# Rows of 128 extra bytes between the split activations and weights of a float32r transformer trunk

## The chip, the cores and the metric

The kernel runs on one core of a Trainium2 chip (trn2). The metric is the device time of one execution in microseconds (us). Two runs of the kernel before took 1998.0 and 1999.53 us, median 1998.76 us. TensorE (PE) multiplies, VectorE (DVE) and ScalarE (ACT) work elementwise, GpSimd (POOL) does a few elementwise steps, and SyncE (SP) issues all DMAs.

## The reference, cut to what matters

Two layers of a bidirectional encoder on 512 tokens of width 1024, all in float32. Each layer is FFN, token mixing, FFN, each behind an RMS norm with a shift, a scale and a gate that come from a conditioning vector.

```python
def swiglu(h, wi, wo):
    gate, up = jnp.split(h @ wi, 2, axis=-1)
    return (jax.nn.silu(gate) * up) @ wo
...
    for l in range(DEPTH):
        mod = (c_act @ ada_w[l] + ada_b[l]).reshape(b, N_MOD, 1, D_MODEL)
...
        h = modulate(rmsnorm(x, norm_ffn1[l]), sh1, sc1)
        x = x + 0.5 * g1 * swiglu(h, ffn1_wi[l], ffn1_wo[l])
        h = modulate(rmsnorm(x, norm_mix[l]), sh2, sc2)
        x = x + g2 * token_mixing(h, cos, sin, w_in[l], sink[l], onorm_a[l], onorm_b[l], w_out[l])
        h = modulate(rmsnorm(x, norm_ffn2[l]), sh3, sc3)
        x = x + 0.5 * g3 * swiglu(h, ffn2_wi[l], ffn2_wo[l])
    return rmsnorm(x, final_norm)
```

`token_mixing` projects h to queries, keys and values (`w_in`), attends in 16 heads, and projects back (`w_out`). D_FF is 2816, that is 22 tiles of 128.

## The kernel before

Activations lie feature-major: a tile holds 128 features in its partitions and the 512 tokens along the row. Each float32 operand of a large product is split into two float32r parts, a high one and the rest, and `mm3` makes a product of three matmuls: high weight by high activation (line 149), low weight by high activation (line 150), high weight by low activation (line 151). The weights are stationary (a load of 128x128, which the trace shows apart as PEld, one per matmul), the activations are the moving operand.

The tiles in question are these:

- `hi` and `lo` (lines 124, 125 and 736): the two parts of one weight chunk, 1024 float32r per partition, six buffers each in the pool `wp`. A chunk holds up to 8 stationary blocks of 128 columns, so its blocks lie 512 bytes apart.
- `hh0..7` and `hl0..7` (lines 209, 210): the two parts of the normed activations, 512 columns, one buffer each in the pool `hp`. They are moving operands of the FFN's first product and of the mixer's projections. In the projection of the values (lines 451 to 453) it is the other way round: `hi` and `lo` move, 320 columns at a time, and `hh`, `hl` are stationary.
- `gh0..7` and `gl0..7` (lines 361, 362): the two parts of the gated activations of the FFN, 512 columns, in the pool `ffn` that is opened anew for each FFN. They are the moving operands of the FFN's second product.

`yh` and `yl` (line 641) are the attention's second half; they take the slots of `hh` and `hl` in `hp`, with 512 columns. `yah` and `yal` (line 648) are the first half, in the pool `mix`.

Within a pool the tiles lie one behind the other. Their rows are 4096 or 2048 bytes, whole multiples of 512, so all tiles of a pool begin at the same remainder. In the program as built, `hi`, `lo`, `hh` and `hl` begin at multiples of 256 bytes (`hi` at 53504, 57600, ..., `hh0` at 102656), and all tiles of the pools `ffn` and `mix` begin 128 bytes beyond one (`gh0` at 188032).

An FFN runs in three thirds of 7, 7 and 8 hidden tiles: first the products with `wi`, whose two results give `gh` and `gl` of a hidden tile (`take`), then the eight output tiles (`out_tiles`). Where a norm follows, the last output tiles and the first tiles of the next phase (`group`) run by token halves, 256 columns at a time. Each engine runs its instructions in the order in which the scheduler wrote them.

Of the kernel before, what the change touches and what calls it, by code (L numbers as in the profile page):

```python
# [11 lines left out]
F32R = mybir.dt.float32r  # L12
# [6 lines left out]
KD = 8  # L19
# [39 lines left out]
def tile_trunk(ctx: ExitStack, tc: tile.TileContext, xT, c, positions, adaT, cols, sink, wi1, wo1,  # L59
# [25 lines left out]
    snk = const.tile([128, L * 8], F32, name="snk")  # L85
    nsnk = const.tile([128, L * 8], F32, name="nsnk")

    # weight stream: every chunk is loaded once, in the order of use, and split into two float32r parts
    specs = []
    finer = set()  # L90
    live = {}
# [24 lines left out]
    def emit_chunk(pieces=1):  # L116
        i = state["emit"]
        if i >= len(specs):
            return
        state["emit"] += 1  # L120
        ap = specs[i]
        n = ap.shape[1]
        raw = wp.tile([128, 1024], F32, tag="raw", name="raw", bufs=2)
        hi = wp.tile([128, 1024], F32R, tag="hi", name="hi")
        lo = wp.tile([128, 1024], F32R, tag="lo", name="lo")
        nc.sync.dma_start(raw[:, :n], ap)
        step = 512 if i in finer else n
        for a in range(0, n, step):
            sl = slice(a, min(a + step, n))
            A.activation(hi[:, sl], raw[:, sl], AF.Copy)  # L130
            V.tensor_tensor(lo[:, sl], raw[:, sl], hi.bitcast(F32)[:, sl], op=ALU.subtract)  # L131
        live[i] = (hi, lo)
# [21 lines left out]
    HALF = (slice(0, HS), slice(HS, S))  # L154

    def rsqrt(out, src, n, scale):
        """(src * scale + EPS) ** -0.5: an integer guess and two steps of third order; the constant factor of
        both steps is in the argument."""
        v, t, y, q = (tiny.tile([128, 8], F32, tag=f"r{i}", name=f"r{i}")[:, :n] for i in range(4))
        V.tensor_scalar(v, src, scale * RK, EPS * RK, op0=ALU.mult, op1=ALU.add)  # L160
        V.tensor_scalar(y.bitcast(I32), v.bitcast(I32), -0.5, float(0x5F3759DF), op0=ALU.mult, op1=ALU.add)
        for ca, cb, o in ((RA, RB, y), (RA / RQ, RB / RQ ** 2, out)):
            V.tensor_tensor(t, y, y, op=ALU.mult)
            V.tensor_tensor(t, t, v, op=ALU.mult)
            V.scalar_tensor_tensor(q, t, -ca, t, op0=ALU.add, op1=ALU.mult)
            V.scalar_tensor_tensor(o, q, cb, y, op0=ALU.add, op1=ALU.mult)
# [3 lines left out]
    class Norm:  # L170
# [35 lines left out]
            self.R[h] = p  # L206

        def alloc(self):
            self.h = [(hp.tile([128, S], F32R, tag=f"hh{k}", name=f"hh{k}"),
                       hp.tile([128, S], F32R, tag=f"hl{k}", name=f"hl{k}")) for k in range(KD)]  # L210

        def make(self, k, h, gs, sh, s=None):
            s = s or HALF[h]
# [8 lines left out]

    temps = [None, None]

    # adaLN: one column of the modulation per 128 outputs
    ada_list = []
    ada = {}

# [46 lines left out]
        ada["cs"] = cs  # L275

    def group(norm, gs, sh, n):
        """First n output tiles of a phase, contraction outermost, so that they follow the norm."""
        Ws = [chunk() for _ in range(n)]
        ps = [pm.tile([128, S], F32, tag="mm", name="mm") for _ in range(n)]  # L280
        if not norm.h:
            norm.alloc()
        for k in range(KD):
            if k >= norm.made:
                norm.make(k, 0, gs, sh)
            for W, p in zip(Ws, ps):
                mm3(p[:, HALF[0]], W, k, norm.h[k], HALF[0], k == 0, k == KD - 1)
            if k == KG[0]:
                with tc.high_priority(offset=HG):
                    norm.stat(1)  # L290
            if k == KG[1]:
                norm.bcast(1)
        for k in range(KD):
            norm.make(k, 1, gs, sh)
        for W, p in zip(Ws, ps):
            for k in range(KD):
                mm3(p[:, HALF[1]], W, k, norm.h[k], HALF[1], k == 0, k == KD - 1)
            yield p
            ahead()
# [7 lines left out]

    def out_tiles(jobs, kts, X, gate, norm, step=None, skew=SKEW, at=((0, 5), (2, 3)),
                  final=None, mod=None):
        """jobs: (m, weights, first k tile of them). The last ones run by token halves when a norm follows."""  # L310
        n = len(jobs)
        for q in range(n - skew if norm else n):
            m, W, w0 = jobs[q]()
            p = pm.tile([128, S], F32, tag="mm", name="mm")
            for k in range(kts):
                mm3(p, W, w0 + k, X[k], FULL, k == 0, k == kts - 1)
            resid(p, m, gate, FULL, norm, None, final)
            ahead()
            if step:
                step()  # L320
        if norm:
            last = [jobs[q]() for q in range(n - skew, n)]
            ps = [pm.tile([128, S], F32, tag="mm", name="mm") if q < 4 else
                  pq.tile([128, S], F32, tag="s", name="mm") for q in range(skew)]
            ahead(AH)
            for h in range(2):
                for j, (m, W, w0) in enumerate(last):
                    for k in range(kts):
                        if h == 1 and (j, k) == at[0]:
                            with tc.high_priority(offset=HP):  # L330
                                norm.stat(0)
                        if h == 1 and (j, k) == at[1] and not final:
                            norm.bcast(0)
                            norm.alloc()
                            for m2 in range(PRE):
                                norm.make(m2, 0, *mod)
                                norm.made += 1
                        mm3(ps[j][:, HALF[h]], W, w0 + k, X[k], HALF[h], k == 0, k == kts - 1)
                    with tc.high_priority(offset=HP):
                        with tc.issue_after(norm.first) if h and j == skew - 1 and norm.made else nullcontext():  # L340
                            resid(ps[j], m, gate, HALF[h], norm, h if j == skew - 1 and h in TAIL[bool(final)] else None, final)

    def ffn(l, sub, norm, pool, step, start=None, final=None, mod=None):
# [3 lines left out]
        for ti, (f0, n) in enumerate(THIRDS):  # L347
# [3 lines left out]
            def take(p):  # L351
                pend.append(p)
                if len(pend) < 2:
                    return
                pg, pu = pend
                pend.clear()
                sg = pool.tile([128, S], F32, tag="sg", name="sg", bufs=2)
                A.activation(sg, pg, AF.Silu)  # L358
                V.tensor_tensor(sg, sg, pu, op=ALU.mult)  # L359
                j = len(g)  # L360
                gh = pool.tile([128, S], F32R, tag=f"gh{j}", name=f"gh{j}")
                gl = pool.tile([128, S], F32R, tag=f"gl{j}", name=f"gl{j}")
                A.activation(gh, sg, AF.Copy)  # L363
                V.tensor_tensor(gl, sg, gh.bitcast(F32), op=ALU.subtract)  # L364
                g.append((gh, gl))
# [25 lines left out]
    def mixer(l, norm, pool, mod):  # L391
# [150 lines left out]
                yield n  # L542

        def heads_(makers, after):
            """The heads' steps, each head's scores a head ahead of its values."""
            cur = makers[0]()
            for qt in range(4):
                cur.scores(qt)
# [19 lines left out]
                cur = nxt  # L568

        def weave(main, fills):  # L570
            """Steps of main with fills[i] = (first head, generator, us of it per step) from that head on."""
            due = 0.0
            i = 0
            for n in main:
                if i + 1 < len(fills) and n >= fills[i + 1][0]:
                    for _ in fills[i][1]:
                        pass
                    i += 1
                    due = 0.0
                due += fills[i][2]  # L580
                while due > 0:
                    d = next(fills[i][1], None)
                    if d is None:
                        break
                    due -= d
            for _ in fills[i][1]:
                pass
# [106 lines left out]
        out_tiles(jobs(), 4, ya, gate, nxt, None, MSK, MAT, mod=mod)  # L694
        return nxt

    # ---- start
    FP = dict(bufs=1, reuse_waits="tile")
    first = ctx.enter_context(ExitStack())
    pool = first.enter_context(tc.tile_pool(name="ffn", **FP))  # L700
# [3 lines left out]
    make_identity(nc, ident)  # L704

    def warm(n):
        """Products that nobody reads: the array's clock follows its activity."""
        p = pm.tile([128, S], F32, tag="mm", name="warm")
        for _ in range(n):
            T.matmul(p[:, :128], ident, ident, start=True, stop=True)  # L710
# [19 lines left out]
    def start():  # L730
        n = 6
        Ws = []
        for j in range(n):
            raw = wp.tile([128, 1024], F32, tag="raw", name="raw", bufs=2) if j < 2 else \
                pool.tile([128, 1024], F32, tag=f"raw{j}", name="raw")
            hi, lo = (wp.tile([128, 1024], F32R, tag=t, name=t) if j < 6 else
                      pool.tile([128, 1024], F32R, tag=t, name=t) for t in ("hi", "lo"))
            Ws.append((raw, hi, lo))
        ps = [pm.tile([128, S], F32, tag="mm", name="mm") if j < 4 else pq.tile([128, S], F32, tag="s", name="mm")
              for j in range(n)]  # L740
# [61 lines left out]
        ada_step()  # L802
    first.close()
    def final_out(norm, xgs, pool):
        """The last norm: the tiles with their gain go back to token-major and take the tokens' factors there."""
        for h in range(2):
            ps = []
            for t in range(2):
# [133 lines left out]
```

## Time and profile before

| what | value |
|---|---|
| median of two runs | 1998.76 us |
| span of the profiled execution, first to last instruction | 1996.3 us |
| PE busy | 98% of the span, 10016 matmuls |
| DVE, ACT, POOL busy | 59%, 38%, 5% |
| mean granted TensorE clock | 0.995 of full speed |

The profiled execution's own time is its span, and the median of the runs is 2.5 us longer; work ahead of the first and behind the last instruction lies in that difference. A matmul's record starts when its moving operand begins to stream and ends when its last result is out, so records of neighbours overlap. The time that a matmul costs in a stream is therefore the distance from its start to the next one's start, called the spacing below, and not the length of its record.

### The profile page before, as it was taken

The page shows a single profiled execution, that of the slowest core. Times are in us where ns is not written, and L with a number is a line of the kernel's source. Part 1 is how long each engine was busy: PE and PEld are TensorE (multiplying, and loading weights), DVE is VectorE, ACT ScalarE, POOL GpSimd, SP SyncE. Part 2 cuts the span into 40 slices and gives each one's busy share as a digit, 9 for nine tenths or more (in the row PEclk, how much of TensorE's full clock was granted, in tenths as well). Part 3 has the DMA queues.
Part 4 walks back from the last instruction along what each step waited for, and adds up shares of the span by engine and source line. Part 5 has one row for each costly group of instructions (what it writes and reads, how often), then busy time and mean ns, then how long its engine had stood idle before and what let it go on. Part 6 is the DMA issues. An engine that isn't in the chain of part 4 may idle for free.

```text
span 1996.3 us, 25904 instructions
## 1 busy us (share of the span) xinstructions
PE 1965.7 (98%) x10016; PEld 1654.3 (83%) x10016; DVE 1169.7 (59%) x2130; ACT 750.9 (38%) x1332; POOL 91.8 (5%) x69
## 2 busy tenths in 40 slices
PE   7999999999999999999999999999999999999998
PEld 5888888898778888888898888889877898888887
DVE  7978433576798888733473333337678973333333
ACT  4422222355685422222242222224557752222223
POOL 4000000021200000000000000000121000000000
PEclk8999999999999999999999999999999999999999
DMA  7788333244413698633233223331543123332331
GB/s 255 277 302 330 132 100 101 84 109 122 126 38 112 219 332 322 238 96 104 85 96 92 98 96 97 100 98 59 153 110 102 54 77 101 102 97 92 104 95 43
DMA packets 84942, 266.97 MB, mean 134 GB/s; under 512 B 10706, under 2 KB 13906, under 8 KB 84820
## 3 DMA queue, kind: packets, MB, share of 16 engines
q1 hardware_dynamic: 84820, 265.33, 40.8%
q8 instruction: 79, 1.29, 0.3%
q14 instruction: 43, 0.35, 0.0%
HBM read 244.31 MB, written 2.10 MB: 123 GB/s over the span
## 4 chain that ended last, share of the span: by engine, by line
PE 90%; DVE 4%; DMA 2%; issue 2%; ACT 1%; SPq 0%; POOL 0%; DVEq 0%; ACTq 0%; POOLq 0%
PE mm L151 26%; PE mm L149 26%; PE mm L150 26%; PE ptr L512 2%; PE po L519 1%; PE po L520 1%; PE s L482 1%; PE s L483 1%; DVE lo L131 1%; PE mm L451 1%; PE mm L453 1%; PE mm L452 1%; PE p L527 1%; DVE araw L236 1%; DMA qs<-t 1%
## 5 line engine op out<-in xcount | busy, mean ns | idle before, releaser
L149 PE MATMUL mm<-hh,hi 128*128 128x512 f32 (+1 forms) x1776 | 662.2, 374 | 6.7 <-ACT hh L219 6.7
L151 PE MATMUL mm<-hl,hi 128*128 128x512 f32 (+1 forms) x1776 | 659.4, 373 | 2.3 <-DVE hl L220 2.2
L150 PE MATMUL mm<-hh,lo 128*128 128x512 f32 (+1 forms) x1776 | 661.5, 373 | 0.0
L130 ACT ACTIVATE hi<-raw 128x1024 fp32r<-128x1024 f32 (+5 forms) x365 | 334.9, 927 | 672.9 <-PE mm L151 569.7
L131 DVE TENSOR_TENSOR lo<-raw,hi 128x1024 fp32r<-128x1024 f32 (+5 forms) x365 | 396.9, 1093 | 306.7 <-ACT hi L130 304.6
L149 PEld LDWEIGHTS mm<-hh,hi 128*128 128x128 f32 x1776 | 336.1, 189 | 65.3 <-ACT hh L219 8.0
L151 PEld LDWEIGHTS mm<-hl,hi 128*128 128x128 f32 x1776 | 335.5, 189 | 61.4 <-DVE hl L220 3.9
L150 PEld LDWEIGHTS mm<-hh,lo 128*128 128x128 f32 x1776 | 335.5, 189 | 57.0
L151 PE MATMUL mm<-gl,hi 128*128 128x512 f32 (+1 forms) x832 | 299.7, 360 | 0.3 <-DVE gl L364 0.3
L150 PE MATMUL mm<-gh,lo 128*128 128x512 f32 (+1 forms) x832 | 299.9, 360 | 0.0
L149 PE MATMUL mm<-gh,hi 128*128 128x512 f32 (+1 forms) x832 | 299.8, 360 | 0.0
L302 DVE SCALAR_TENSOR_TENSOR x<-mm,fin,x 128x512 f32<-128x512 f32 (+1 forms) x156 | 101.8, 652 | 207.1 <-PE mm L151 206.9
L236 DVE CUSTOM_DVE_ANT_0 araw<-araw,cs 128x1024 f32<-128x1024 f32 x136 | 166.8, 1236 | 32.2 <-DMA araw<-in_adaT_dram 31.1
L151 PEld LDWEIGHTS mm<-gl,hi 128*128 128x128 f32 x832 | 156.3, 188 | 26.9 <-DVE gl L364 0.8
L149 PEld LDWEIGHTS mm<-gh,hi 128*128 128x128 f32 x832 | 156.3, 188 | 26.4 <-ACT gh L363 0.2
L150 PEld LDWEIGHTS mm<-gh,lo 128*128 128x128 f32 x832 | 156.4, 188 | 26.2
L358 ACT ACTIVATE sg<-mm 128x512 f32<-128x512 f32 x88 | 52.5, 598 | 271.6 <-PE mm L151 269.1
L359 DVE TENSOR_TENSOR sg<-sg,mm 128x512 f32<-128x512 f32 x88 | 60.3, 686 | 158.6 <-PE mm L151 157.0
L404 POOL TENSOR_TENSOR part<-part,rs 128x512 f32<-128x512 f32 x26 | 34.5, 1326 | 1282.8 <-DVE part L402 1280.5
L491 ACT ACTIVATE sm<-sm,nb 128x512 f32<-128x512 f32 (+2 forms) x128 | 81.6, 638 | 30.0 <-DVE nb L487 30.0
L512 PE MATMUL ptr<-ident,sm 128*128 128x128 f32 x416 | 81.5, 274 | 0.9 <-DVE pl L516 0.9
L516 DVE TENSOR_TENSOR pl<-ptr,ph 128x512 fp32r<-128x512 f32 (+2 forms) x128 | 73.2, 584 | 8.6 <-ACT ph L515 7.8
(141 smaller groups left out, 1789.9 us busy)
## 6 DMA issues: line engine op xcount, KB each, us to landing
raw<-in_wi_dram SPq DMA_DIRECT2D x170, 512.0 KB, 3.5
araw<-in_adaT_dram SPq DMA_DIRECT2D x144, 512.0 KB, 5.5
raw<-in_wo_dram SPq DMA_DIRECT2D x64, 448.0 KB, 3.3
raw<-in_wo_dram SPq DMA_DIRECT2D x32, 512.0 KB, 3.5
raw<-in_wqk_dram SPq DMA_DIRECT2D x26, 512.0 KB, 3.5
raw<-in_w_out_dram SPq DMA_DIRECT2D x16, 512.0 KB, 3.5
kh<-qh SPq DMA_DIRECT2D x40, 128.0 KB, 2.3
kl<-t SPq DMA_DIRECT2D x40, 128.0 KB, 2.3
```

The lines of the kernel that those rows point to most:

```text
L130: A.activation(hi[:, sl], raw[:, sl], AF.Copy)
L131: V.tensor_tensor(lo[:, sl], raw[:, sl], hi.bitcast(F32)[:, sl], op=ALU.subtract)
L149: T.matmul(ps, wh, X[0][:, s], start=start, stop=False)
L150: T.matmul(ps, wl, X[0][:, s], start=False, stop=False)
L151: T.matmul(ps, wh, X[1][:, s], start=False, stop=stop)
L236: return V.tensor_tensor_reduce(out=raw, in0=raw, in1=ada["cs"], scale=1.0, scalar=0.0, op0=ALU.mult, op1=ALU.add, accum_out=mod[:, l, ch, ...
L302: V.scalar_tensor_tensor(x[:, m, s], ps[:, s], gate[:, m:m + 1], x[:, m, s], op0=ALU.mult, op1=ALU.add)
L358: A.activation(sg, pg, AF.Silu)
L359: V.tensor_tensor(sg, sg, pu, op=ALU.mult)
L491: A.activation(s[:, :w], s[:, :w], AF.Exp, scale=-1.0, bias=self.nb[:, qt:qt + 1], accum_out=self.den[:, qt:qt + 1])
L512: T.transpose(p[:, j * 128:j * 128 + 128], self.sm[qt][:, c0:c0 + 128], ident)
L516: V.tensor_tensor(pl[:, :w], p[:, :w], ph.bitcast(F32)[:, :w], op=ALU.subtract)
```

## The change

The tiles `hi`, `lo`, `hh`, `hl`, `gh` and `gl` are allocated with 32 more columns of four bytes, and only the first 1024 or 512 columns are used. The rows are then 4224 and 2176 bytes, an odd multiple of 128 bytes, so each tile begins 128 bytes further on, counted within 256 or 512 bytes, than the one ahead of it. `yh`, `yl`, `yah`, `yal` and the other tiles of the mixer keep their 2048 bytes. To make room, the scratch that is kept free in each partition for software-made DMA descriptors shrinks from 16384 to 1024 bytes. The branch for more than six chunks in `start`, where n is 6, goes, and comments and texts of functions go.

```diff
@@ emit_chunk
-        hi = wp.tile([128, 1024], F32R, tag="hi", name="hi")
-        lo = wp.tile([128, 1024], F32R, tag="lo", name="lo")
+        hi = wp.tile([128, 1056], F32R, tag="hi", name="hi")[:, :1024]
+        lo = wp.tile([128, 1056], F32R, tag="lo", name="lo")[:, :1024]
@@ Norm.alloc
-            self.h = [(hp.tile([128, S], F32R, tag=f"hh{k}", name=f"hh{k}"),
-                       hp.tile([128, S], F32R, tag=f"hl{k}", name=f"hl{k}")) for k in range(KD)]
+            self.h = [(hp.tile([128, S + 32], F32R, tag=f"hh{k}", name=f"hh{k}")[:, :S],
+                       hp.tile([128, S + 32], F32R, tag=f"hl{k}", name=f"hl{k}")[:, :S]) for k in range(KD)]
@@ ffn, take
-                gh = pool.tile([128, S], F32R, tag=f"gh{j}", name=f"gh{j}")
-                gl = pool.tile([128, S], F32R, tag=f"gl{j}", name=f"gl{j}")
+                gh = pool.tile([128, S + 32], F32R, tag=f"gh{j}", name=f"gh{j}")[:, :S]
+                gl = pool.tile([128, S + 32], F32R, tag=f"gl{j}", name=f"gl{j}")[:, :S]
@@ start
-            hi, lo = (wp.tile([128, 1024], F32R, tag=t, name=t) if j < 6 else
-                      pool.tile([128, 1024], F32R, tag=t, name=t) for t in ("hi", "lo"))
+            hi, lo = (wp.tile([128, 1056], F32R, tag=t, name=t)[:, :1024] for t in ("hi", "lo"))
@@ kernel
-    nc = _bacc.Bacc("TRN2", target_bir_lowering=False, num_devices=1)
+    nc = _bacc.Bacc("TRN2", target_bir_lowering=False, num_devices=1, dynamic_dma_scratch_size=1024)
```

Each engine's instructions and their order are the same in both programs. In the changed one the six buffers of `hi` begin at 38144, 42368, 46592 and so on, in turn at a multiple of 256 bytes and 128 beyond one; `lo` goes in step with `hi`. All `hh` begin at a multiple of 256 and all `hl` 128 beyond one; all `gh` begin 128 beyond one and all `gl` at one.

## Rows read from the trace of the kernel before

**Rows 1.** The page: busy time of TensorE, and shares of the chain of waits.
```profile
PE 1965.7 (98%) x10016; PEld 1654.3 (83%) x10016; DVE 1169.7 (59%) x2130; ACT 750.9 (38%) x1332; POOL 91.8 (5%) x69
...
PE 90%; DVE 4%; DMA 2%; issue 2%; ACT 1%; SPq 0%; POOL 0%; DVEq 0%; ACTq 0%; POOLq 0%
```

**Rows 2.** Groups of TensorE's matmuls by line and form: count, busy, mean, idle before.
```profile
L149 PE MATMUL mm<-hh,hi 128*128 128x512 f32 x1456 | 572.7, 393 | 6.7 <-ACT hh L219 6.7
...
L149 PE MATMUL mm<-gh,hi 128*128 128x512 f32 x576 | 227.5, 395 | 0.0
...
L149 PE MATMUL mm<-hh,hi 128*128 128x256 f32 x320 | 89.5, 285 | 0.0
...
L149 PE MATMUL mm<-gh,hi 128*128 128x256 f32 x256 | 72.3, 282 | 0.0
...
L451 PE MATMUL mm<-hi,hh 128*128 128x320 f32 x128 | 40.7, 318 | 1.8 <-DVE t L403 1.8
...
L149 PE MATMUL mm<-yh,hi 128*128 128x512 f32 x64 | 26.1, 408 | 0.4 <-ACT yh L613 0.4
```

**Rows 3.** Timeline of TensorE, first FFN, second third, product with hh, 512 columns.
```profile
190.23 0.39 PE L149 MATMUL mm<-hh,hi 128*128 128x512 f32 x1
...
226.95 0.39 PE L149 MATMUL mm<-hh,hi 128*128 128x512 f32 x1
```

**Rows 4.** Timeline of TensorE, the output tiles that follow, 512 columns.
```profile
227.63 0.40 PE L149 MATMUL mm<-gh,hi 128*128 128x512 f32 x1
...
228.32 0.39 PE L149 MATMUL mm<-gh,hi 128*128 128x512 f32 x1
228.55 0.40 PE L150 MATMUL mm<-gh,lo 128*128 128x512 f32 x1
228.79 0.39 PE L151 MATMUL mm<-gl,hi 128*128 128x512 f32 x1
...
266.59 0.39 PE L151 MATMUL mm<-gl,hi 128*128 128x512 f32 x1
```

**Rows 5.** Timeline of TensorE, 256 columns: output tiles, then the mixer's first group.
```profile
380.07 0.28 PE L151 MATMUL mm<-gl,hi 128*128 128x256 f32 x1
...
388.97 0.28 PE L151 MATMUL mm<-gl,hi 128*128 128x256 f32 x1
...
403.65 0.28 PE L149 MATMUL mm<-hh,hi 128*128 128x256 f32 x1
...
407.97 0.28 PE L149 MATMUL mm<-hh,hi 128*128 128x256 f32 x1
```

**Rows 6.** Timeline of TensorE in the opening, first products with hh, 512 columns.
```profile
20.83 0.63 PE L149 MATMUL mm<-hh,hi 128*128 128x512 f32 x1
...
24.25 0.63 PE L150 MATMUL mm<-hh,lo 128*128 128x512 f32 x1
...
24.99 0.39 PE L149 MATMUL mm<-hh,hi 128*128 128x512 f32 x1
25.21 0.39 PE L150 MATMUL mm<-hh,lo 128*128 128x512 f32 x1
...
26.14 0.40 PE L151 MATMUL mm<-hl,hi 128*128 128x512 f32 x1
```

**Rows 7.** Windows: stretch, length, each engine's busy time (instructions), PEclk, DMA share, GB/s.
```profile
190.00:227.00 37.00, 37.00 (x165) 30.64 (x164) 23.72 (x37) 10.52 (x15) 0.00 (x0) 1.00 0.57 198
...
700.00:721.00 21.00, 21.00 (x94) 17.40 (x93) 18.30 (x29) 6.06 (x8) 0.00 (x0) 1.00 0.93 339
...
20.90:24.90 4.00, 4.00 (x11) 3.13 (x10) 4.00 (x2) 0.88 (x1) 4.00 (x3) 0.51 0.41 144
```

**Rows 8.** The page: the groups that write hi and lo.
```profile
L130 ACT ACTIVATE hi<-raw 128x1024 fp32r<-128x1024 f32 (+5 forms) x365 | 334.9, 927 | 672.9 <-PE mm L151 569.7
L131 DVE TENSOR_TENSOR lo<-raw,hi 128x1024 fp32r<-128x1024 f32 (+5 forms) x365 | 396.9, 1093 | 306.7 <-ACT hi L130 304.6
```

**Rows 9.** The page: the DMA queue that carries the kernel's data.
```profile
q1 hardware_dynamic: 84820, 265.33, 40.8%
```

## The prediction

> **What bounds the kernel now.** I read the page first: TensorE is busy in 98% of the span, and the chain of waits lies on it for 90% [rows 1]. So what counts is how fast TensorE's stream runs, and I read that from the distance between the starts of neighbouring matmuls in the timeline. In the first FFN's second third the products with `hh` and `hl` go from 190.23 to 226.95 us in 162 steps [rows 3]: 36.72 / 162 = 226.7 ns each. The output tiles behind them, with `gh` and `gl`, go from 227.63 to 266.59 us in 167 steps [rows 4]: 38.96 / 167 = 233.3 ns, and there long and short steps take turns (228.32, 228.55, 228.79: 0.23 and 0.24 us). Both streams have the same instructions, the same 512 columns and the full clock. The reader is to see that two streams of one form differ by 6.6 ns a step.
>
> Where does the difference come from? At half the granted clock (0.51, which is the lower level, 1.2 GHz, while the stream had only just begun [rows 7]) the steps with `hh` are (24.25 - 20.83) / 8 = 427 ns [rows 6], which is 512 columns at one per cycle of that clock and nothing more. At the upper level 512 columns alone would be half of it, 213.3 ns. So at full clock a step carries 13 ns extra with `hh` and 20 ns with `gh`. Another engine is not the cause: around 700 us DVE is busy 18.30 of 21.00 us and 94 matmuls fall into the stretch, in the stretch of rows 3 it is busy 23.72 of 37.00 us and 165 do [rows 7]; that is 223 and 224 ns for each record counted, the same within what the edges of a stretch add. What is left of the differences that I can see are the addresses. A weight load runs beside each matmul, so at any time two streams read the SBUF for TensorE. The tiles `hh` and the weights begin at the same remainder of 256 bytes, `gh` and the weights 128 bytes apart. I take the address difference between the moving row and the weight block that is loaded beside it as the cause of the 6.6 ns. That is an inference from two stages, not something that a row shows by itself.
>
> **The change part by part.** *Offsets.* The order of instructions stays, so only the pairs of offsets change. Before, nearly every pair with `hh` is aligned (difference a multiple of 256) and every pair with `gh` is 128 apart. After, the weights' six buffers alternate between both remainders, and of the three matmuls of a product `hi`, `lo`, `hi` have one remainder and `hh`, `hh`, `hl` two. Counted over the program, half the pairs are aligned and half are 128 apart, with `hh` as with `gh`. If a step's cost follows its pair, both streams come to (226.7 + 233.3) / 2 = 230.0 ns. A second look at the same value: just after the clock rose, aligned pairs that have not yet settled run from 24.99 to 26.14 us in 5 steps [rows 6], 230 ns each. A stream whose offsets change at every third step has no time to settle, so I take 230 for it, and not one of the settled values.
>
> The sum, for the 512-column matmuls, from the counts [rows 2], each of the three lines having as many as the one shown: with `hh`, 3 x 1456 = 4368, with `yh`, 3 x 64 = 192, together 4560 x (230.0 - 226.7) = +15.0 us. With `gh`, 3 x 576 = 1728 x (230.0 - 233.3) = -5.7 us.
>
> *256 columns.* With `gh` 75 steps take 388.97 - 380.07 = 8.90 us, 118.7 ns; with `hh` 36 steps take 407.97 - 403.65 = 4.32 us, 120.0 ns [rows 5]. Here it is the pairs that are 128 apart that are faster. Half and half is 119.35: 3 x 320 = 960 x -0.65 = -0.6 us and 3 x 256 = 768 x +0.65 = +0.5 us [rows 2]. Together nothing.
>
> *320 columns, the value projection.* 3 x 128 = 384 matmuls [rows 2]; before nearly all pairs are aligned, after half are not. No row has the other kind in this form. The nearest are the 512 columns (+6.6 ns for such a pair) and the 256 columns (-1.3): -0.2 to +1.3 us when half of the 384 change. I take +1.3, the end of the longer form, which is nearer to a full row.
>
> *The stream's neighbours.* The rows that write `hi` and `lo` take 927 and 1093 ns, 334.9 and 396.9 us in all [rows 8]. If other offsets made them 10% longer or shorter, that is 40 us on DVE, which is busy 59%, and 33 us on ACT, at 38% [rows 1], beside TensorE's stream; three chunks are split ahead of their use, so it stays hidden, and I put it at nothing. Its cover would go only where DVE is the full engine, around 700 us, 87% [rows 7]; 20 chunks there by 0.1 us is 2 us, kept for the range.
>
> *Scratch and the dropped branch.* All data moves through the hardware's queue [rows 9], no queue of GpSimd's stands in the page, so a smaller scratch takes nothing away. The branch is never entered with n = 6. Nothing for both. The attention's own products (`kh`, `qs`, `ph`, `v2`) keep their places among each other.
>
> Sum: +15.0 - 5.7 + 0 + 1.3 = +10.6 us. TensorE's stream has no other slack to give, so it goes to the end: span 1996.3 + 10.6 = 2006.9, and with the 2.5 us between span and median 2009.
>
> *A rule against.* The rows show 13 to 20 ns a step over the columns' time. The Trainium skill, TensorE: Matmul & The Clock Gate, section "Back-to-back issue gap", gives N / 1.2 ns at the low clock, which agrees with the 427 ns here, and N / 2.4 + 2.5 ns at the high one for a single gap, 215.8 for 512 columns; the trace has 226.7 and 233.3 in its place. By that figure some 11 to 17 ns a step would be a clash that offsets might remove, an estimate of about -100 us over all these matmuls; it is the first rival's mechanism. The Trainium skill, SBUF — State Buffer, section "Who interferes with whom", says that TensorE's two read ports are independent and that TensorE never waits on anyone; by that rule the change does nothing and the time stays at 1999, which is the third rival, and the two stages of rows 3 and 4 speak against it.
>
> **The rivals.** *The clash goes.* If each new offset kept the two streams apart, the spacing would fall to the columns' 213.3 ns. The mean of the 512-column matmuls above is (4560 x 226.7 + 1728 x 233.3) / 6288 = 228.5, so 6288 x 15.2 = 96 us, and at 256 columns 1728 x (119.4 - 106.7) = 22 us: 1881. For it speaks that the extra is nil at the low clock, so it is no fixed price of a step. Against it, that 128 apart is one of the offsets that come, and it is slower, not faster, at 512 columns; the shortest step in the unsettled rows is 0.22 us (24.99 to 25.21 [rows 6]), and the 2% begin at 228.5 - 40 / 6.288 = 222.1.
>
> *It settles low.* With offsets that vary, each step might settle at 226.7, or the streams might drift to the short steps of 224 or so: 1728 x -6.6 = -11 us gives 1987, 6288 x -4.5 = -28 us gives 1970.
>
> *Addresses do nothing.* Then 233.3 against 226.7 is something else about the output stage, and the time stays at 1999. Against: lines, forms and clock are the same. What would make it so: a wait for PSUM or a start order that the trace doesn't show.
>
> *The long step stays.* In the output tiles every second step takes 0.24 us [rows 4], some 238 ns. If offsets that change at each step made nearly every step a long one, 6288 x (238 - 228.5) = +60 us: 2059. It decides from a mean of 234.9 on (+40 us). Against: long and short steps are seen in turn only, and their mean has not been over 233.3.
>
> **How the numbers follow.** A measurement of this kernel tells about 2% from no change, 40 us, so 1959 to 2039 counts as same. Mixed offsets at about the mean of both kinds, 1999 to 2031: 0.57 (2031 is all 512-column pairs at 233.3, 4560 x 6.6 = 30 us, and the 320 columns). Settles low, 1965 to 1999: 0.22. Addresses do nothing: 0.08. The clash goes, beyond 2%: 0.08. The long step, beyond 2%: 0.05. The predicted time is the first's, 2009. The range from 1975 to 2032 leaves out the two cases beyond 2% and the lowest end of the second. Faster 0.08, same 0.87, slower 0.05.
>
> **What the new profile would show.** Steps with `hh` at 512 columns near 230 ns in place of 226.7, and no longer equal; steps with `gh` near 230 in place of 233.3; the 256-column steps as before; the same counts and order, and the groups that write `hi` and `lo` at 0.93 and 1.09 us. A spacing that is longest where chunk and activation are 128 apart shows the pair as cause. The prediction is wrong if the difference that matters is not 128 in 256 bytes but a finer or coarser one, for which the trace of before has no row, or if it isn't the pair that counts but the moving row's own place.

## The result

The changed kernel takes 2012.11 us (median of two runs, 2010.74 to 2013.48) against 1998.76: the ratio is 1.0062, with a 95% interval from 1.0043 to 1.0081. It is slower by 13.4 us, which is clear of noise and within the 2% that count as the same. 2009 had been forecast, with a range from 1975 to 2032. The profiled execution's span went from 1996.3 to 2008.9 us, +12.6.

The page of the changed kernel: busy time, the queue, and the groups that write `hi` and `lo`.

```profile
PE 1978.7 (98%) x10016; PEld 1653.0 (82%) x10016; DVE 1171.1 (58%) x2130; ACT 750.4 (37%) x1332; POOL 91.6 (5%) x69
...
q1 hardware_dynamic: 84820, 265.33, 41.7%
...
L130 ACT ACTIVATE hi<-raw 128x1024 fp32r<-128x1024 f32 (+5 forms) x365 | 334.9, 927 | 677.0 <-PE mm L151 586.2
L131 DVE TENSOR_TENSOR lo<-raw,hi 128x1024 fp32r<-128x1024 f32 (+5 forms) x365 | 397.1, 1094 | 317.5 <-ACT hi L130 315.9
```

Against [rows 1, 8, 9]: TensorE has the same 10016 matmuls and is busy 13.0 us longer, beside 12.6 us of span, so the difference is there. Every other engine's busy time is the same within 1.4 us; the groups that write to the padded rows take 927 and 1094 ns as before. So the change is in TensorE's stream alone, and the timeline shows where. First the first FFN's second third, as in [rows 3, 4]: the first matmul of the products with `hh`, of the output tiles, and of the third behind them.

```profile
151.74 0.40 PE L149 MATMUL mm<-hh,hi 128*128 128x512 f32 x1
...
229.34 0.39 PE L149 MATMUL mm<-gh,hi 128*128 128x512 f32 x1
...
268.20 0.40 PE L149 MATMUL mm<-hh,hi 128*128 128x512 f32 x1
```

In the kernel before, the same three matmuls stand at these times:

```profile
151.42 0.40 PE L149 MATMUL mm<-hh,hi 128*128 128x512 f32 x1
...
227.63 0.40 PE L149 MATMUL mm<-gh,hi 128*128 128x512 f32 x1
...
266.82 0.39 PE L149 MATMUL mm<-hh,hi 128*128 128x512 f32 x1
```

336 steps with `hh` take 77.60 us, 231.0 ns each in place of 226.8 (76.21 us), and 168 steps with `gh` take 38.86 us, 231.3 in place of 233.3 (39.19 us). Within this mean the chunks differ. The same timeline, the first matmul of three chunks with `hh` and of three with `gh`:

```profile
184.94 0.39 PE L149 MATMUL mm<-hh,hi 128*128 128x512 f32 x1
...
190.54 0.40 PE L149 MATMUL mm<-hh,hi 128*128 128x512 f32 x1
...
196.04 0.39 PE L149 MATMUL mm<-hh,hi 128*128 128x512 f32 x1
...
239.06 0.40 PE L149 MATMUL mm<-gh,hi 128*128 128x512 f32 x1
...
243.87 0.39 PE L149 MATMUL mm<-gh,hi 128*128 128x512 f32 x1
...
248.77 0.40 PE L149 MATMUL mm<-gh,hi 128*128 128x512 f32 x1
```

A chunk of 24 steps takes 5.60 us, the next 5.50: 233.3 and 229.2 ns. With `gh`, 21 steps take 4.81 and 4.90 us: 229.0 and 233.3. Every second chunk's buffer lies 128 bytes beyond a multiple of 256, and the two values take turns with it: all 22 chunks of the stretch lie at 229.0 to 229.7 ns or at 233.3 to 233.4. The first chunk with `hh` is the exception: by the turns it belongs at 233.3 and runs at 229.2. The same happens wherever the first chunk behind a change of operand is of that kind, in ten places of this trace, this one among them. That no chunk runs at 230.0 ns, the mean of the two old values, is the first thing that the prediction did not have.

### The profile page after: what moved, and what is told of

It is laid out like the page before. It is cut to its first block, busy times and chain, and to the rows that moved or that the text cites. A ratio compares the mean times of both kernels' runs of the same rounds, so it can differ in the third digit from the quotient of the medians.

```text
span 2008.9 us, 25901 instructions
## 1 busy us (share of the span) xinstructions
PE 1978.7 (98%) x10016; PEld 1653.0 (82%) x10016; DVE 1171.1 (58%) x2130; ACT 750.4 (37%) x1332; POOL 91.6 (5%) x69
## 4 chain that ended last, share of the span: by engine, by line
PE 92%; DVE 3%; DMA 1%; issue 1%; ACT 1%; POOL 0%; SPq 0%; DVEq 0%; ACTq 0%; POOLq 0%
PE mm L150 27%; PE mm L149 27%; PE mm L151 27%; PE ptr L512 2%; PE po L519 1%; PE po L520 1%; PE s L482 1%; PE s L483 1%; PE mm L451 1%; PE mm L453 1%; PE mm L452 1%; PE p L527 1%; DMA qs<-t 0%; DVE lo L131 0%; DVE araw L236 0%
## 5 line engine op out<-in xcount | busy, mean ns | idle before, releaser
L150 PE MATMUL mm<-hh,lo 128*128 128x512 f32 (+1 forms) x1776 | 668.5, 377 | 0.0
L131 DVE TENSOR_TENSOR lo<-raw,hi 128x1024 fp32r<-128x1024 f32 (+5 forms) x365 | 397.1, 1094 | 317.5 <-ACT hi L130 315.9
L150 PEld LDWEIGHTS mm<-gh,lo 128*128 128x128 f32 x832 | 156.6, 188 | 24.8
```

The source lines that it names most:

```text
L150: T.matmul(ps, wl, X[0][:, s], start=False, stop=False)
```

## The experiments

Each kernel of the model's work keeps every engine's instructions and their order; only places in SBUF differ, but for the last kind, where two matmuls of a product change places. Times are medians; in the first four the kernel before took 1999.07 us beside them (21 runs), in the next three 1999.18 (7 runs). The two spacings are those of the stretch above, each worked out from the same three rows.

| kernel | offset of hh / gh against the weights | us | ratio to before, 95% interval | hh, gh, ns a step |
|---|---|---|---|---|
| before | 0 / 128 | 1998.76 | | 226.8, 233.3 |
| changed | both, varying | 2012.11 | 1.0062 [1.0043, 1.0081] | 231.0, 231.3 |
| e1_align | 0 / 0 | 1987.62 | 0.9942 [0.9929, 0.9954] | 226.7, 226.7 |
| e2_hh_apart | 128 / 0 | 2013.13 | 1.0070 [1.0056, 1.0083] | 233.3, 226.8 |
| e3_all_shift | 0 / 128, all moved | 1999.12 | 0.9995 [0.9986, 1.0004] | 226.8, 233.3 |
| e4_pad256 | 0 / 128, padded by 256 | 1998.56 | 0.9999 [0.9990, 1.0008] | 226.7, 233.3 |
| e5_weights | changes from chunk to chunk | 2007.01 | 1.0038 [1.0023, 1.0053] | 230.1, 229.8 |
| e6_acts | changes within a product | 2017.05 | 1.0091 [1.0074, 1.0108] | 233.3, 228.9 |
| e9_reuse | 0 / 0, other order | 1987.33 | 0.9939 [0.9924, 0.9954] | 226.7, 226.7 |

**Is it the offset, and which?** Four kernels. The first takes the kernel before and puts one tile of 128 bytes ahead of the pools that are opened later:

```diff
     tiny = ctx.enter_context(tc.tile_pool(name="tiny", bufs=4))
+    ctx.enter_context(tc.tile_pool(name="gap", bufs=1)).tile([128, 32], F32, name="gap")
     pm = ctx.enter_context(tc.tile_pool(name="pm", bufs=4, space=PSUM))
```

> The kernel before, with one tile of 128 bytes allocated behind the pool tiny, so that every tile of the pools ffn and mix begins at a multiple of 256 bytes, as the weights and hh do. No row is padded. Theory (the pair of moving row and weight block counts, and a constant aligned pair settles at 226.7 ns): the 512-column steps with gh go from 233.3 to 226.7 ns, -11.7 us with yah; the 256-column steps with gh and yah go from 118.7 to 120.0, +1.4 us; together -10.3 us, a median of about 1988.5 us. Rival (the output stage is slower for another reason than addresses): gh stays at 233.3, 1998.8 us. Rival (any two offsets that differ are better than equal ones): not faster than before.

Measured: 1987.62 us, ratio 0.9942. The timeline of the aligned kernel, the same three matmuls:

```profile
150.44 0.39 PE L149 MATMUL mm<-hh,hi 128*128 128x512 f32 x1
...
226.60 0.39 PE L149 MATMUL mm<-gh,hi 128*128 128x512 f32 x1
...
264.68 0.39 PE L149 MATMUL mm<-hh,hi 128*128 128x512 f32 x1
```

The output tiles now take 38.08 us for 168 steps, 226.7 ns, the same as the products ahead of them. So the output stage was never slow by itself: 128 bytes of empty space moved it. This kernel is faster than both the kernel before and the changed one.

The second puts the same tile between the weights' pool and that of `hh`:

```diff
     wp = ctx.enter_context(tc.tile_pool(name="wp", bufs=6))
+    ctx.enter_context(tc.tile_pool(name="gap", bufs=1)).tile([128, 32], F32, name="gap")
     hp = ctx.enter_context(tc.tile_pool(name="hp", bufs=1))
```

> The kernel before, with one tile of 128 bytes allocated between the pools wp and hp: hh, hl, yh and yl now lie 128 bytes off the weights, gh and gl are aligned with them. The two streams have changed places. Theory: hh at 512 columns goes from 226.7 to about 233.3 ns (4560 steps, +30 us), gh to 226.7 (-11.7 us), 256 columns about even: +18.5 us, about 2017 us. Rival (the output stage is slower by itself): nothing changes with the offset, 1998.8 us.

Measured: 2013.13 us. The timeline, the same three matmuls:

```profile
151.39 0.40 PE L149 MATMUL mm<-hh,hi 128*128 128x512 f32 x1
...
229.78 0.39 PE L149 MATMUL mm<-gh,hi 128*128 128x512 f32 x1
...
267.88 0.40 PE L149 MATMUL mm<-hh,hi 128*128 128x512 f32 x1
```

The products with `hh` take 78.39 us, 233.3 ns, the output tiles 38.10 us, 226.8. The two streams have changed places, and the time grew by 14.1 us, where 18.5 had been expected (15.1 in the span of the profiled execution). Summed from start to start over both traces, `gh` at 512 columns fell by 11.7 us, as forecast, but `hh` and `yh` grew by 24.8 us in place of 30: a step of `hh` that nothing holds up gained 6.0 ns and not 6.6, and `yh` gained next to nothing. The 320-column matmuls of the value projection, which this forecast left out, are busy 122.9 us in place of 120.9: with every pair 128 apart that form is dearer too.

The third puts it ahead of the weights, so that all move together:

```diff
     const = ctx.enter_context(tc.tile_pool(name="const", bufs=1))
+    ctx.enter_context(tc.tile_pool(name="gap", bufs=1)).tile([128, 32], F32, name="gap")
     wp = ctx.enter_context(tc.tile_pool(name="wp", bufs=6))
```

> The kernel before, with one tile of 128 bytes allocated between the pools const and wp: weights, hh, gh and all that follows are moved by 128 bytes together, so that every pair keeps its difference, but hh is now 128 bytes beyond a multiple of 256 and gh at one. Theory (the pair counts): nothing changes, 226.7 and 233.3 ns, 1998.8 us. Rival (the moving row's own place counts): hh goes to 233.3 and gh to 226.7, +18.5 us, about 2017 us.

Measured: 1999.12 us, 226.8 and 233.3 ns. The rival, by which the moving row's own place counts, falls.

The fourth takes the changed kernel with 1088 columns in place of 1056 and S + 64 in place of S + 32:

```diff
-        hi = wp.tile([128, 1056], F32R, tag="hi", name="hi")[:, :1024]
+        hi = wp.tile([128, 1088], F32R, tag="hi", name="hi")[:, :1024]
```

> The changed kernel with 256 bytes of padding in place of 128: each tile lies at another offset within 512 bytes and more, but within 256 bytes all is as in the kernel before (hh aligned, gh 128 apart). Theory (only the difference within 256 bytes counts): 226.7 and 233.3 ns again, about 1998.8 us. Rival (the difference within 512 bytes or more counts, or offsets that vary keep the stream from settling): hh near 231 ns as in the changed kernel, about 2015 us.

Measured: 1998.56 us, 226.7 and 233.3 ns. The tiles now lie at different offsets within 512 bytes, but at the same one within 256, and the spacings are those of before. This kernel has the small scratch and the dropped branch too, so neither costs anything that can be measured, as forecast.

**Does each step pay for its own pair, or does the pattern count?** The changed kernel, once with only the weights padded (S in place of S + 32), once with only the activations (1024 in place of 1056). The first two lines of the cut are of the one kernel, the last two of the other.

```diff
-            self.h = [(hp.tile([128, S + 32], F32R, tag=f"hh{k}", name=f"hh{k}")[:, :S],
+            self.h = [(hp.tile([128, S], F32R, tag=f"hh{k}", name=f"hh{k}")[:, :S],
...
-        hi = wp.tile([128, 1056], F32R, tag="hi", name="hi")[:, :1024]
+        hi = wp.tile([128, 1024], F32R, tag="hi", name="hi")[:, :1024]
```

> The changed kernel with only the weights' rows padded: within one chunk every pair has the same offset, from chunk to chunk it changes between aligned and 128 apart. If a step costs what its pair costs when the pair stays the same: half of the 512-column steps at 226.7 and half at 233.3 ns, with hh as with gh, about 2009 us. If a stream needs some steps to settle after each change of offset, the aligned chunks start above 226.7 and the time is 1 to 3 us more, 2010 to 2012.

> The changed kernel with only the activations' rows padded: every product has both offsets, for hh two aligned pairs and one 128 apart, for gh the other way round. If a step costs what its pair costs: hh at 228.9, gh at 231.1 ns, 4560 x 2.2 - 1728 x 2.2 = +6 us, about 2005 us. If offsets that change within a product keep the stream from settling, so that a step costs about 231 whatever its own pair: hh +4.3, gh -2.3 ns, +16 us, about 2014 us.

Measured: 2007.01 and 2017.05 us. With the weights alone, 230.1 and 229.8 ns: with `hh` the chunks take 227.4 and 232.9 ns in turn. The aligned ones start with steps of 228 to 233 ns and are at 226.7 from the fourth on, so where the offset stays the same for a chunk, a step does cost about what its pair costs; the time is 2 us under the lower of the two forecasts. The activations alone decide between the theories. The timeline of that kernel:

```profile
153.07 0.40 PE L149 MATMUL mm<-hh,hi 128*128 128x512 f32 x1
...
231.47 0.39 PE L149 MATMUL mm<-gh,hi 128*128 128x512 f32 x1
...
269.93 0.40 PE L149 MATMUL mm<-hh,hi 128*128 128x512 f32 x1
```

With `hh`, where two of three pairs are aligned, a step takes 78.40 / 336 = 233.3 ns, as much as if none were. With `gh`, where two of three are 128 apart, it takes 38.46 / 168 = 228.9, less than the mean of its pairs. Both theories fall: where offsets change within a product, a step does not pay for its pair, and neither do mixed streams all run at some 231. What counts is the pattern of offsets that repeats.

**The map of offsets.** A kernel that does none of the model's work and only streams products from two tiles:

```python
    def run(name, offs, n, count, fixed=False):
        p = pp.tile([128, 512], F32, tag="p", name=name)
        for i in range(count):
            o = offs[i % len(offs)] // 4
            w = 0 if fixed else i % 8 * 128
            T.matmul(p[:, :n], W[:, w:w + 128], X[:, o:o + n], start=i == 0, stop=i == count - 1)
        return p
```

> None of the model's work: streams of 48 products from two SBUF tiles alone, one stream for each offset of the moving row against the weight block, in steps of 32 bytes from 0 to 480 at 512 columns (fulla to fullp) and from 0 to 224 at 256 columns (halfa to halfh); four with one weight block throughout (fixeda to fixedd: 0, 64, 128, 192 bytes); two with offsets 0, 0, 128 and 128, 128, 0 in turn (mixa, mixb); one at 16 bytes (fine). Theory: 226.7 ns at 0 and 256 and about 233 at 128 and 384, repeating every 256 bytes; the mixed ones near 231. What lies between is open: with a distance that counts, values between the two; if only the same start settles, about 231 to 233 at every other offset. Rival (other engines' traffic makes the 6.6 ns): one value for all offsets, since no other engine works here. A spacing under 226.7 at any offset would show a better layout than the aligned one.

Its timeline has one row for each stream of 48; a step is the distance to the next row's start, over 48.

```profile
22.22 11.04 PE L77 MATMUL fulla<-X,W 128*128 128x512 f32 x48
33.10 11.37 PE L77 MATMUL fullb<-X,W 128*128 128x512 f32 x48
44.30 11.16 PE L77 MATMUL fullc<-X,W 128*128 128x512 f32 x48
55.30 11.37 PE L77 MATMUL fulld<-X,W 128*128 128x512 f32 x48
66.51 11.36 PE L77 MATMUL fulle<-X,W 128*128 128x512 f32 x48
77.71 11.40 PE L77 MATMUL fullf<-X,W 128*128 128x512 f32 x48
88.95 11.35 PE L77 MATMUL fullg<-X,W 128*128 128x512 f32 x48
...
111.33 11.05 PE L77 MATMUL fulli<-X,W 128*128 128x512 f32 x48
122.22 11.37 PE L77 MATMUL fullj<-X,W 128*128 128x512 f32 x48
...
200.45 5.91 PE L77 MATMUL halfa<-X,W 128*128 128x256 f32 x48
206.20 5.82 PE L77 MATMUL halfb<-X,W 128*128 128x256 f32 x48
211.85 5.82 PE L77 MATMUL halfc<-X,W 128*128 128x256 f32 x48
217.51 5.91 PE L77 MATMUL halfd<-X,W 128*128 128x256 f32 x48
223.26 5.86 PE L77 MATMUL halfe<-X,W 128*128 128x256 f32 x48
...
245.98 11.09 PE L77 MATMUL fixeda<-X,W 128*128 128x512 f32 x48
256.91 11.17 PE L77 MATMUL fixedb<-X,W 128*128 128x512 f32 x48
...
290.27 11.36 PE L77 MATMUL mixa<-X,W 128*128 128x512 f32 x48
301.47 11.16 PE L77 MATMUL mixb<-X,W 128*128 128x512 f32 x48
312.46 11.28 PE L77 MATMUL fine<-X,W 128*128 128x512 f32 x48
```

At 512 columns: offset 0 takes 226.7 ns, 32 takes 233.3, 64 takes 229.2, 96 takes 233.5, 128 takes 233.3, 160 takes 234.2, and 256 (`fulli`) is at 226.9 again; the eight streams from 256 to 480 bytes repeat the eight from 0 to 224 within 0.2 ns. No other engine works here, so traffic of other engines is not needed for it, and the model's 226.7 and 233.3 come back from two tiles. The mixed streams answer the last experiment: 0, 0, 128 takes 11.20 / 48 = 233.3 ns, and 128, 128, 0 takes 10.99 / 48 = 229.0. Those are the two values of the chunks in the changed kernel. At 256 columns the order is another: aligned takes 119.8 ns, 32 and 64 bytes 117.7 and 117.9, 96 bytes 119.8. With one weight block throughout (`fixeda`), the aligned stream takes 10.93 / 48 = 227.7 ns, its first steps being longer; from the middle on it runs at 226.7 too, so that the block changes is no part of the extra.

**Can a load be saved?** Two matmuls in a row with the same weight block, on top of the aligned kernel:

```diff
-        T.matmul(ps, wl, X[0][:, s], start=False, stop=False)
-        T.matmul(ps, wh, X[1][:, s], start=False, stop=stop)
+        T.matmul(ps, wh, X[1][:, s], start=False, stop=False)
+        T.matmul(ps, wl, X[0][:, s], start=False, stop=stop)
```

> The aligned kernel (first experiment) with the three matmuls of each product in another order: high weight by high activation, high weight by low activation, low weight by high activation, so that two matmuls in a row have the same weight block. If the program loads the block again each time, the loads stay at 10016 and the time at about 1988 us. If the second load falls away and the extra 13 ns belong to a load's reading, a third of the 512-column steps fall from 226.7 towards 216: 6288 / 3 x 11 = 23 us less, about 1965 us.

Measured: 1987.33 us, no difference from the aligned kernel. The page has 10016 loads (PEld), so the second load is made again; in the sweep, too, `fixeda` has 48 loads for its 48 products. A stream without a load for each matmul was not seen, so what the loads cost stays open.

**Is the extra the load's reading?** The same streams with narrower blocks, W[:, w:w + cols] into p[:cols, :n], and finer offsets:

> None of the model's work: streams of 48 products at 512 columns from two SBUF tiles alone, as in the sweep. The weight block is 128, 96, 64 or 32 columns wide (wa to wd), with the moving row aligned (even) and 128 bytes apart (apart); then finer offsets of 4, 8, 16, 24, 48, 80 and 240 bytes (offa to offg) with the full block. If the extra 13.3 ns are the price of the load's reading beside the stream, they shrink with the block: about 226.7, 223.3, 220.0 and 216.7 ns for the aligned streams, and the difference between aligned and apart shrinks too. Rival (a fixed price of changing the weights): 226.7 ns at every width. The fine offsets: if only the same start in 256 bytes settles early, 230 to 234 ns at each; an offset under 226.7 would be a better layout.

```profile
22.38 11.04 PE L76 MATMUL waeven<-X,W 128*128 128x512 f32 x48
33.26 11.35 PE L76 MATMUL waapart<-X,W 128*128 128x512 f32 x48
44.45 11.22 PE L76 MATMUL wbeven<-X,W 128*96 128x512 f32 x48
55.51 11.27 PE L76 MATMUL wbapart<-X,W 128*96 128x512 f32 x48
66.62 11.21 PE L76 MATMUL wceven<-X,W 128*64 128x512 f32 x48
77.67 11.27 PE L76 MATMUL wcapart<-X,W 128*64 128x512 f32 x48
88.77 11.27 PE L76 MATMUL wdeven<-X,W 128*32 128x512 f32 x48
99.88 11.23 PE L76 MATMUL wdapart<-X,W 128*32 128x512 f32 x48
110.95 11.53 PE L76 MATMUL offa<-X,W 128*128 128x512 f32 x48
122.31 11.38 PE L76 MATMUL offb<-X,W 128*128 128x512 f32 x48
```

The aligned streams take 226.7, 230.4, 230.2 and 231.5 ns for blocks of 128, 96, 64 and 32 columns: a narrower block makes a step longer, not shorter, though the record of its load falls from 188 ns at 128 columns to 109 at 32. Neither the price of reading the block nor a fixed price of 13.3 ns fits. Aligned and apart do come together (6.5 ns between them at 128 columns, 1.0 at 64, -0.8 at 32), so of these two offsets the full block alone shows a clear difference. At 4 bytes a step takes 236.7 ns, the longest of all; the other six fine offsets take 230.2 to 233.8, and none is under 226.7.

**Which block does a row meet?** The blocks' offsets go 0, 0, 128 in turn, and the rows' follow the block of their own, of the next or of the one after. In each call the rows' offsets stand first, then the blocks':

```python
    Z, H = 0, 128
    ...
    run("own", (Z, Z, H), (Z, Z, H))
    run("next", (Z, H, Z), (Z, Z, H))
    run("third", (H, Z, Z), (Z, Z, H))
    run("both", (H,), (H,))
    run("weight", (Z,), (H,))
```

> None of the model's work: streams of 60 products at 512 columns from two SBUF tiles alone. Which weight block does a moving row meet? The blocks' offsets go 0, 0, 128 in turn, and the rows' offsets are those of their own block (own), of the next one, which is loaded beside them (next), or of the one after (third). Theory: next settles at 226.7 ns, the other two don't (229 to 233). Rival (a row meets its own block): own settles at 226.7. Then rows and blocks both 128 off (both): 226.7; blocks alone 128 off (weight): 233 if the sign of the difference doesn't matter; and rows in turn at 0 and 128 (turna), 0 and 64 (turnb), 0, 0, 64 (turnc), 64, 64, 0 (turnd), 64, 64, 128 (turne) with blocks at 0: between 228 and 234, none under 226.7.

```profile
21.44 14.04 PE L77 MATMUL own<-X,W 128*128 128x512 f32 x60
35.32 14.04 PE L77 MATMUL next<-X,W 128*128 128x512 f32 x60
49.20 13.90 PE L77 MATMUL third<-X,W 128*128 128x512 f32 x60
62.94 13.79 PE L77 MATMUL both<-X,W 128*128 128x512 f32 x60
76.57 14.15 PE L77 MATMUL weight<-X,W 128*128 128x512 f32 x60
90.56 13.96 PE L77 MATMUL turna<-X,W 128*128 128x512 f32 x60
```

Over 60 steps: own 231.3 ns, next 231.3, third 229.0, both 227.2 with its settling, weight alone 233.2. None of the three that follow a block comes to 226.7, the one that the theory named as little as the others. With the full block, 226.7 as a lasting value was seen only where every row and every block start at the same remainder of 256 bytes. The turns of two offsets took 230.0 to 233.3 ns; rows at 0 and 128 in turn (`turna`) do come to the mean of their pairs, 13.80 / 60 = 230.0.

## Why the prediction came out right

**The bound and the place.** Right. All of the loss is in TensorE's stream, nothing in ACT, DVE, the scratch or the branch, and the difference counts within 256 bytes. That the two stages differ by their addresses was an inference; with one empty tile the difference goes or changes sides, so it is now shown. Offsets finer than 128 bytes count as well (229.2 ns at 64), but this change makes none. The loads do not run "at any time": their records fill 83% of the span [rows 1].

**The step's cost.** "If a step's cost follows its pair, both streams come to (226.7 + 233.3) / 2 = 230.0 ns": the value was near, the reason wrong. Chunks run at 233.3 or at 229.2 ns by the repeating pattern of offsets, and half of each kind makes 231.2, near the 231.0 and 231.3 of the stretch. That this lies 1.2 ns from the mean of the pairs is luck: with the activations alone padded, the mean of the pairs gives 2005 us, and 2017.05 was measured. The prediction's second reason, that a stream with varying offsets has no time to settle, fares no better: such a stream comes to a steady pattern, only at another value. The sign that was to show the pair as cause, the longest spacing where chunk and activation are 128 apart, came out the other way: with two of three pairs aligned a step takes 233.3 ns, with two of three 128 apart 229.0, in the kernel with padded activations as in the streams `mixa` and `mixb`.

**The sum.** Over the steps of both traces that nothing held up (under 300 ns), `hh` went from 227.0 to 231.2 ns at 512 columns, 4368 x 4.2 = +18.3 us, and `yh` from 228.9 to 230.9, 192 x 2.0 = +0.4, where +15.0 had been put for both; `gh` from 233.2 to 231.0, 1728 x -2.2 = -3.8 where -5.7 had been. The 256-column steps with `hh` fell from 121.0 to 119.7, -1.2 us where -0.6 had been put, those with `gh` from 119.6 to 119.3, -0.2 in place of +0.5. The 320 columns gave nothing, where +1.3 was expected (their three groups stay at 120.9 us busy, to a tenth). Together +13.5, beside +12.6 measured in the span and +13.4 in the medians. The forecast of +10.6 was low mainly by the step, put at 230.0 where it took 231.

**The rivals.** Addresses do nothing: refuted by the first two experiments. The clash goes: none of 15 offsets within 256 bytes that were tried at 512 columns runs under 226.7 ns. The figure for a single gap by the formula of the Trainium skill, TensorE: Matmul & The Clock Gate, section "Back-to-back issue gap", 215.8 ns for 512 columns, was reached in no stream here, in which each matmul has a load. It settles low: possible, but by making all offsets equal, not different; the aligned kernel's 1987.6 us is that rival's first figure. The long step stays: 236.7 ns at 4 bytes is the nearest to it. The rule of the Trainium skill, SBUF — State Buffer, section "Who interferes with whom", that TensorE's two read ports are independent and that TensorE never waits on anyone, does not foresee this: with no other engine at work, the streams `fulla` and `fulle` differ by 6.6 ns with the place of their rows against the blocks.

**Open.** Why equal starts run at 226.7 ns and others do not, by which rule a repeating pattern comes to its value (the first chunk behind a change of operand shows that what ran before it counts too), and why narrower blocks cost more (they also fill fewer rows of the result, which was not tried apart), is not explained by these runs; the theory that a moving row meets the block that is loaded beside it has fallen, and nothing has taken its place.

## What to carry to other kernels

Read the spacing of matmuls from start to start, by stage: two stages with the same form and clock but another spacing can point to where their tiles lie. With float32r operands and a weight load for each matmul, let all moving rows and weight blocks of a 512-column stream start at the same remainder of 256 bytes; within a pool, tiles whose rows are multiples of 256 bytes do that by themselves, but another pool can begin elsewhere, and one small tile ahead of it can undo it or mend it (1987.6 against 1999.1 us here). Padding to spread tiles over offsets is not a gain by itself, and a mean over kinds of pairs is no safe model where a stream's pattern repeats.

## What the runs showed of the hardware that was not expected

- The spacing of 512-column float32r matmuls with a load each has a period of 256 bytes in the offset between row and block: 226.7 ns at 0 and 256, 229.2 at 64, 233.1 to 234.2 at the other multiples of 32, 236.7 at 4 bytes. A common shift of all tiles by 128 bytes changes nothing. At 256 columns the aligned stream, at 119.8 ns, is among the slowest.
- With all blocks at one offset, a stream with two aligned rows in three takes 233.3 ns, one with a single aligned row in three 229.0.
- Weight blocks of 96, 64 and 32 columns, aligned, give 230.4, 230.2 and 231.5 ns where the full block gives 226.7.
- For two matmuls in a row with the same block these programs load it twice: 10016 loads for 10016 matmuls.
